# Modulation weight units of a two-layer diffusion backbone: in rows at four places, or one by one among gates, merge and up projection

## The chip, the core and the metric

The kernel runs on one core of a Trainium2 chip. The metric is the device time of one execution in microseconds (us). The engines are TensorE (PE in the rows; PEld is its weight load), VectorE (DVE), ScalarE (ACT), GpSimd (POOL) and SyncE (SP, which issues nearly all DMAs). All arithmetic is float32; a matmul product is made from high and low parts in three terms (high x high, low x high, high x low), so every weight block of 512 KB is split once into `wh` (ScalarE) and `wl` (VectorE).

## The reference, cut to what matters

Six vectors per layer (shift, scale and gate of each of the two sub-layers) are a product of SiLU of the condition with `w_mod`, for the latent and for the context tokens. They depend on nothing else, so they can be computed at any time before their first use.

```python
for l in range(DEPTH):                                   # DEPTH = 2, 512 latent and 256 context tokens
    mod_l = jnp.split((silu_c @ w_mod[l] + b_mod[l])[:, None, :], 6, axis=-1)
    mod_c = jnp.split(silu_cc @ w_mod[l] + b_mod[l], 6, axis=-1)
    pl = split_proj(modulate(x, mod_l[0], mod_l[1]) @ w_in[l] + b_in[l])
    ...
    mix_l = gated_merge(pl[-1], yr_l, ya_l, ym_l, w_br_ret[l], w_br_att[l], w_br_mlstm[l], w_out[l])
    x = layer_norm(alpha * x + mod_l[2] * mix_l, ln1_g[l], ln1_b[l])
    ffn_l = conv_ffn(modulate(x, mod_l[3], mod_l[4]), w_up[l], conv_w[l], conv_b[l], w_down[l])
    x = layer_norm(alpha * x + mod_l[5] * ffn_l, ln2_g[l], ln2_b[l])
```

The context tokens go the same way in layer 0; in layer 1 only the latent tokens go past the mixers.

## The kernel before

**The modulation units.** `w_mod` of both layers is cut into 48 units (layer, which of the six vectors, which quarter). One unit (`mod_unit`, L332) loads two raw blocks of 512 KB from `wmod` and makes eight matmuls of 256 columns into the tile `pp`, four in each block, with the raw weights as the moving side and 32 columns of the condition (`silc`) as the fixed side. The result is copied by ScalarE (first of four units) or added by VectorE (the other three) into `part`, 128 x 256, L345 and L348. When four units are in `part`, the next unit, or a demand for one of the four, calls `flush_mod` (L319): two small matmuls into `pm` turn `part` into columns, and four VectorE instructions (L328) write them to `modc`. The first eight units run at the very start and in the first projection. The other 40 wait in the list `modq`, in the order of layer, vector and quarter. `tmod(l, idx, n)` (L353) takes up to n of them off the list if they are not past (l, idx); `need_mod` (L358) takes all up to (l, idx) and flushes.

**The order of the work.** TensorE's order is the order in which the program is written; the `Mixer` lets background generators (the scans, attention, `finish`, `gate_rows`) step in between the matmul groups of the foreground by an estimated clock. The order on the other engines and on SyncE's queue is made by a scheduler that keeps dependencies. Raw blocks lie in a ring of five buffers, split blocks in two pairs, PSUM in three banks for the long products (`g`) and five for everything else; each DMA on SyncE's queue waits in its turn for its buffer.

**The stages of a layer.** After the input projections and the scans, 24 gate blocks are projected and stored to DRAM (`dr_g`), with attention in the background. `merge` then runs for three branches, each with four weight blocks (`wbr`); its input, the tile pair `yh`, `yl`, is converted by `yprep` (L1290) from `dr_y` and lies in the same buffer as the input of the gate blocks. The output projection (`wout`) follows, and `finish` (L1045) normalises tile by tile in the background: VectorE and ScalarE make `xn`, then `post` (L1049) transposes it on TensorE (`ptr`) and `to_xT` (L409) modulates it and splits it into `xh` and `xl`, the input of the next projection. The up projection (`wup`, 44 blocks in four groups; context tokens first in the first group) goes through the convolution to `ah`, `al`, and the down projection (`wdn`) of a group follows. A second `finish` makes the input of layer 1.

**Where the 40 units stand.** Eight one by one in the input stage (L1254, L1262, L1269); four at the start of the merge of layer 0 (L1371); in `post` of each of the six tiles two units ahead of the transposes, in the first `finish` of layer 0 (twelve units) and in the second (twelve); in `post` of each of the four tiles of layer 1's first `finish` one unit (four). The numbers stand in the last argument of `finish`: the first two name the vectors that must be there, the other three are the arguments of `tmod`. The `tmod` in the up projection (L1431) finds nothing left that it may take.

Of the kernel before, what the change touches and what calls it, by code (L numbers as in the profile page):

```python
# [149 lines left out]
class Mixer:  # L150
    """Emits the steps of a foreground and of queued background generators in one TensorE order."""

# [51 lines left out]
def _program(es, nc, tc, I, OUT):  # L204
    V, S, G, SP = nc.vector, nc.scalar, nc.gpsimd, nc.sync
    M = Mixer()
# [51 lines left out]
    modc = [ctile([128, 6, 8, 2], f"modc{l}") for l in range(DEPTH)]  # L258
# [786 lines left out]
    def finish(key, X, xslot, gname, bname, l, tiles, emit, xT=None, mc=None, sidx=0, mi=None):  # L1045
# [3 lines left out]
        def post(t, xn):  # L1049
            need_mod(*mi[:2])  # L1050
            tmod(*mi[2:])
            to_xT(xn, t, xT[0], xT[1], mc, sidx, int(t >= 4))
            M.done.add(f"{key}.{t}")
# [55 lines left out]
    def layer(l, xT, key):  # L1109
        last = l == DEPTH - 1  # L1110
# [170 lines left out]
        for f in range(24):  # L1281
            def ev(g, a, b):
                t = stg()
                S.activation(t[:, :b - a], g, AF.Tanh, scale=0.5, bias=bh[:, B_G + f:B_G + f + 1])
                SP.dma_start(out=dr_g[f][:, a:b], in_=t[:, :b - a])
            yield from fm(wblock(I["wfm"][l, B_G - 1 + f]), xh, xl, qseg, ev)

        yh, yl = new_xT()
# [34 lines left out]
        def merge(bi, segs):  # L1323
# [3 lines left out]
            for q in range(4):  # L1327
                blk = wblock(I["wbr"][l, bi, q])
                if bi == 0 and q == 1:
                    yprep(1)  # L1330
                if bi == 1 and yold:
                    yatt_load(yold.pop(0))
                    if yold:
                        yatt_load(yold.pop(0))
# [30 lines left out]
        hT = None  # L1365
# [4 lines left out]
        yprep(0)  # L1370
        tmod(0, 4, 4)  # L1371
        yield from merge(0, qseg)
# [5 lines left out]
        for pi, ats in enumerate(aparts):  # L1378
# [4 lines left out]
            if pi == 0:  # L1383
                X = (zt if last else Xt())[:, :6144].rearrange("p (t c) -> p t c", t=6)
                yield f"g2{l}"
                hT = (yh, yl) if last else new_xT()
                M.add(finish(key, X, xslot, "ln1_g", "ln1_b", l, lt, None, hT, modc[l], 3, (l, 4, 1, 5, 1) if last else (0, 4, 1, 1, 2)), [f"a{l}"])
            for ts in ((ats,) if last else trips):
# [22 lines left out]
        for gr, (go, gnum) in enumerate(zip(GOFF, GROUPS)):  # L1411
# [4 lines left out]
            for pi, segs in enumerate(passes):  # L1416
# [3 lines left out]
                for jn, j in enumerate(range(go, go + gnum)):  # L1420
# [3 lines left out]
                    for half, jj in enumerate((j, NF + j)):  # L1424
# [4 lines left out]
                        tt.append(t)  # L1429
                        if gr and not last:  # L1430
                            tmod(1, 1)  # L1431
                    if cut:
# [13 lines left out]
            if final:  # L1446
# [5 lines left out]
                else:  # L1452
# [3 lines left out]
                    nx = new_xT()  # L1456
                    M.add(finish(key2, X, xslot, "ln2_g", "ln2_b", l, lt, emit, nx, modc[l + 1], 0, (1, 1, 1, 4, 2)))
            if gr == 0:
# [59 lines left out]
```

## Time and profile before

| what | value |
|---|---|
| time, median of three runs | 2564.7 us (2563.7 to 2565.76) |
| span of the profiled execution | 2558.8 us |
| TensorE busy | 2467.1 us, 96% |
| VectorE busy | 1585.4 us, 62% |
| ScalarE busy | 1005.9 us, 39% |
| moved by DMA | 329.21 MB, mean 129 GB/s |

The span goes from the first to the last instruction of one profiled execution; what lies around it is in the time but not in the span. The busy shares are means over stages that differ, so they are read stage by stage: a stretch in which TensorE has no gap, and one in which it waits for another engine, say different things about the same instruction.

### The profile page before, as it was taken

To read this page: it belongs to the slowest core of one execution; us is meant where nothing else is said; L and a number is where in the kernel's file an instruction comes from. 1 tells how busy PE (TensorE), PEld (TensorE's weight loads), DVE (VectorE), ACT (ScalarE), POOL (GpSimd) and SP (SyncE) were. 2 spreads that over 40 slices of the span, in tenths; PEclk is the share of its full clock that TensorE was granted. 3 is DMA by queue.
4 is the path that set the end of the run, shared out by engine and by line. 5 is a ranking of instruction groups with operands and counts; after the bars stand their busy time and mean duration, and the time that the engine had idled before them with its cause. 6 is when DMAs were issued, how large, how long until landed. Compare 5 with 4: busy or idle time off the path is not lost.

```text
span 2558.8 us, 41711 instructions
## 1 busy us (share of the span) xinstructions
PE 2467.1 (96%) x16552; PEld 2163.6 (85%) x16552; DVE 1585.4 (62%) x3338; ACT 1005.9 (39%) x1802; POOL 92.3 (4%) x111
## 2 busy tenths in 40 slices
PE   6999999999899989999999989999999998999998
PEld 4877898888788978999898978778887888988887
DVE  5555465554476885455545684756665778855557
ACT  4422321454443464232313253433245455633332
POOL 1000001000000000000000010000110000000000
PEclk9999999999999999999999999999999999999999
DMA  7343434322454662212121375243443444533232
GB/s 254 102 164 120 144 102 138 113 81 81 150 185 132 227 239 83 83 46 79 54 74 59 95 276 170 91 153 126 158 140 123 139 158 162 182 107 99 83 104 70
DMA packets 147651, 329.21 MB, mean 129 GB/s; under 512 B 15872, under 2 KB 59136, under 8 KB 147456
## 3 DMA queue, kind: packets, MB, share of 16 engines
q1 hardware_dynamic: 147456, 326.54, 38.2%
q8 instruction: 131, 2.15, 0.3%
q14 instruction: 64, 0.52, 0.1%
HBM read 283.49 MB, written 42.99 MB: 128 GB/s over the span
## 4 chain that ended last, share of the span: by engine, by line
PE 86%; DVE 6%; DMA 3%; ACT 3%; issue 1%; POOL 0%; SPq 0%; DVEq 0%; ACTq 0%; POOLq 0%
PE g L214 72%; PE psc L214 2%; PE pAV L214 2%; PE pPT L218 2%; DVE wl L314 1%; PE pNb L214 1%; PE pNf L214 1%; PE pE L214 1%; ACT wh L313 1%; PE pp L214 1%; PE pU L214 1%; PE pO L214 1%; DMA raw<-in_wtm_dram 1%; DMA raw<-in_wmod_dram 1%; DMA stg<-dr_y 1%
## 5 line engine op out<-in xcount | busy, mean ns | idle before, releaser
L214 PE MATMUL g<-xh,wh 128*128 128x512 f32 (+1 forms) x2448 | 825.6, 352 | 11.3 <-ACT xh L1295 5.0
L214 PE MATMUL g<-xl,wh 128*128 128x512 f32 (+1 forms) x2448 | 812.0, 347 | 4.8 <-DVE xl L426 3.7
L314 DVE TENSOR_TENSOR wl<-raw,wh 128x1024 fp32r<-128x1024 f32 (+3 forms) x358 | 411.9, 1151 | 355.7 <-ACT wh L313 267.3
L313 ACT CAST wh<-raw 128x1024 fp32r<-128x1024 f32 (+3 forms) x358 | 355.5, 993 | 609.3 <-PE g L214 550.9
L214 PEld LDWEIGHTS g<-xh,wh 128*128 128x128 f32 x2448 | 465.0, 190 | 82.4 <-issue 12.9
L214 PEld LDWEIGHTS g<-xl,wh 128*128 128x128 f32 x2448 | 465.7, 190 | 61.1 <-DVE xl L426 4.2
L214 PE MATMUL g<-xh,wl 128*128 128x512 f32 (+1 forms) x2448 | 510.2, 347 | 3.0 <-DVE wl L314 3.0
L214 PEld LDWEIGHTS g<-xh,wl 128*128 128x128 f32 x2448 | 401.1, 190 | 61.4 <-DVE wl L314 3.6
L214 PE MATMUL g<-wh,ah 128*128 128x256 f32 x808 | 207.2, 284 | 3.6 <-ACT ah L1439 3.6
L214 PE MATMUL g<-wh,al 128*128 128x256 f32 x808 | 206.4, 283 | 2.7 <-DVE al L1440 2.7
L214 PE MATMUL g<-wh,xh 128*128 128x256 f32 (+1 forms) x768 | 201.1, 292 | 3.0 <-ACT wh L313 2.3
L214 PE MATMUL g<-wh,xl 128*128 128x256 f32 (+1 forms) x768 | 196.8, 287 | 1.6 <-DVE xl L426 1.5
L214 PEld LDWEIGHTS g<-wh,ah 128*128 128x128 f32 x808 | 153.1, 189 | 4.9 <-ACT ah L1439 4.2
L214 PEld LDWEIGHTS g<-wh,al 128*128 128x128 f32 x808 | 153.0, 189 | 4.1 <-DVE al L1440 3.5
L214 PEld LDWEIGHTS g<-wh,xh 128*128 128x128 f32 x768 | 149.0, 194 | 7.6 <-ACT wh L313 2.7
L214 PEld LDWEIGHTS g<-wh,xl 128*128 128x128 f32 x768 | 149.0, 194 | 2.4 <-DVE xl L426 1.9
L1400 ACT ACTIVATE tc<-g,conv 128x512 f32<-128x512 f32 (+1 forms) x142 | 97.0, 683 | 136.8 <-PE g L214 134.9
L927 ACT ACTIVATE Pe<-psc,mx 128x256 f32<-128x256 f32 (+1 forms) x144 | 80.9, 566 | 168.2 <-DVE mx L922 115.9
L214 PE MATMUL g<-wl,ah 128*128 128x256 f32 x808 | 144.0, 281 | 1.3 <-DVE wl L314 1.3
L1401 DVE SCALAR_TENSOR_TENSOR tc<-g,conv,tc 128x511 f32<-128x511 f32 (+1 forms) x142 | 88.7, 625 | 84.5 <-ACT tc L1400 83.9
L398 POOL TENSOR_TENSOR rstd<-veps,mhalf 128x1 f32<-128x1 f32 (+3 forms) x68 | 71.7, 1057 | 1823.4 <-DVE veps L396 1745.9
L214 PE MATMUL g<-wl,xh 128*128 128x256 f32 (+1 forms) x768 | 127.8, 287 | 0.9 <-DVE wl L314 0.8
(279 smaller groups left out, 3199.9 us busy)
## 6 DMA issues: line engine op xcount, KB each, us to landing
raw<-in_wup_dram SPq DMA_DIRECT2D x108, 512.0 KB, 3.5
raw<-in_wmod_dram SPq DMA_DIRECT2D x96, 512.0 KB, 5.4
raw<-in_wfm_dram SPq DMA_DIRECT2D x80, 512.0 KB, 3.4
raw<-in_wtm_dram SPq DMA_DIRECT2D x32, 512.0 KB, 5.1
raw<-in_wout_dram SPq DMA_DIRECT2D x32, 512.0 KB, 3.9
raw<-in_wbr_dram SPq DMA_DIRECT2D x28, 512.0 KB, 3.8
dr_g<-stg SPq DMA_DIRECT2D x48, 256.0 KB, 2.0
raw<-in_wdn_dram SPq DMA_DIRECT2D x20, 512.0 KB, 3.5
```

Source lines behind the costliest of these rows:

```text
L214: nc.tensor.matmul(out, lhsT, rhs, **kw)
L218: nc.tensor.transpose(out, in_, ident)
L313: S.copy(h[:, :n], raw[:, :n])
L314: V.tensor_tensor(l[:, :n], raw[:, :n], h[:, :n].bitcast(F32), op=OP.subtract)
L398: G.tensor_tensor(r, t, mhalf[:, :n], op=OP.pow)
L927: S.activation(pe[:, a:b], prs[si][:, :b - a], AF.Exp, bias=mx[:, 3:4], scale=0.125, accum_out=sm[:, si:si + 1])
L1400: S.activation(t[:, a:b], g, AF.Identity, bias=conv[:, jj, 3:4], scale=conv[:, jj, 1:2])
L1401: V.scalar_tensor_tensor(t[:, a + 1:b], g[:, :b - a - 1], conv[:, jj, 0:1], t[:, a + 1:b], op0=OP.mult, op1=OP.add)
```

## The change

The units behind the first eight that stood in rows are taken one at a time. One is taken after every third gate block of layer 0 (eight), one ahead of every second weight block of a merge of layer 0 (six), and one after each pair of up projection blocks in the groups 1 to 3 of layer 0 (seventeen); the last unit remains for `need_mod` in `gate_rows` of layer 1. The row at the start of the merge and those in `post` are gone. The eight units of the input stage stay.

```diff
@@ class Mixer
-    """Emits the steps of a foreground and of queued background generators in one TensorE order."""
+
@@ finish, post
-            need_mod(*mi[:2])
-            tmod(*mi[2:])
+            need_mod(*mi)
             to_xT(xn, t, xT[0], xT[1], mc, sidx, int(t >= 4))
@@ layer, gate blocks
             yield from fm(wblock(I["wfm"][l, B_G - 1 + f]), xh, xl, qseg, ev)
+            if f % 3 == 2:
+                tmod(0, 5)
@@ layer, merge
                     yprep(1)
+                if not last and q % 2 == 1:
+                    tmod(1, 5)
                 if bi == 1 and yold:
@@ layer, before the first merge
         yprep(0)
-        tmod(0, 4, 4)
         yield from merge(0, qseg)
@@ layer, first finish
-                M.add(finish(key, X, xslot, "ln1_g", "ln1_b", l, lt, None, hT, modc[l], 3, (l, 4, 1, 5, 1) if last else (0, 4, 1, 1, 2)), [f"a{l}"])
+                M.add(finish(key, X, xslot, "ln1_g", "ln1_b", l, lt, None, hT, modc[l], 3, (l, 4)), [f"a{l}"])
@@ layer, up projection
                         tt.append(t)
-                        if gr and not last:
-                            tmod(1, 1)
+                    if gr and not last:
+                        tmod(1, 5)
@@ layer, second finish
-                    M.add(finish(key2, X, xslot, "ln2_g", "ln2_b", l, lt, emit, nx, modc[l + 1], 0, (1, 1, 1, 4, 2)))
+                    M.add(finish(key2, X, xslot, "ln2_g", "ln2_b", l, lt, emit, nx, modc[l + 1], 0, (1, 1)))
```

Three places show how instructions move. TensorE, the start of layer 0's merge, before: `pAV` is the last piece of background attention after the gate blocks, `pp` and `pm` are units and a flush, and the first `g` belongs to the merge.

```order
L218 MATMUL pPT<-ident,Pe 128x128 x6
L214 MATMUL pAV<-PT,va 64x128 x12
L214 MATMUL pp<-raw,silc 32x256 x8
L214 MATMUL pm<-selm,part 128x8 x2
L214 MATMUL pp<-raw,silc 32x256 x24
L214 MATMUL g<-xh,wh 128x512
L214 MATMUL g<-xl,wh 128x512
```

The same place in the changed kernel (the first `g` rows are the end of the last gate block):

```order
L214 MATMUL pAV<-PT,va 64x128 x12
L214 MATMUL g<-xh,wh 128x256
L214 MATMUL g<-xl,wh 128x256
L214 MATMUL g<-xh,wh 128x256
L214 MATMUL g<-xl,wh 128x256
L214 MATMUL g<-xh,wl 128x256 x8
L214 MATMUL pp<-raw,silc 32x256 x8
L214 MATMUL g<-xh,wh 128x512
L214 MATMUL g<-xl,wh 128x512
```

One unit is left between the gates and the merge instead of four, and the flush is gone from there. TensorE, the first tile of layer 0's first `finish`, before: output projection, flush and two units, transposes, output projection.

```order
L214 MATMUL g<-wl,zh 128x256 x4
L214 MATMUL pm<-selm,part 128x8 x2
L214 MATMUL pp<-raw,silc 32x256 x16
L218 MATMUL ptr<-ident,xn 128x128 x8
L214 MATMUL g<-wh,zh 128x256
```

The same place in the changed kernel:

```order
L214 MATMUL g<-wh,zl 128x256
L214 MATMUL g<-wl,zh 128x256 x4
L218 MATMUL ptr<-ident,xn 128x128 x8
L214 MATMUL g<-wh,zh 128x256
L214 MATMUL g<-wh,zl 128x256
```

The transposes now follow the projection directly; so at all 16 tiles. VectorE, the last tile of layer 0's first `finish`, before: `mod` modulates the tile, the two `xl` finish it, `wl` and `tc` belong to the up projection, and `dg` are the diagonal products for the second gate.

```order
L421 TENSOR_SCALAR mod<-ptr,modc_83 128x128 x4
L314 TENSOR_TENSOR wl<-raw,wh 128x1024
L1435 TENSOR_TENSOR tc<-tc 128x256
L314 TENSOR_TENSOR wl<-raw,wh 128x1024
L426 TENSOR_TENSOR xl<-mod,xh 128x4x128
L373 TENSOR_TENSOR dg<-ident,modc_83 128x512 x4
L426 TENSOR_TENSOR xl<-mod,xh 128x4x128
```

The same place in the changed kernel:

```order
L421 TENSOR_SCALAR mod<-ptr,modc_83 128x128
L1404 SCALAR_TENSOR_TENSOR tc<-g,conv,tc 128x255
L314 TENSOR_TENSOR wl<-raw,wh 128x1024
L426 TENSOR_TENSOR xl<-mod,xh 128x4x128 x2
L373 TENSOR_TENSOR dg<-ident,modc_83 128x512 x4
L1403 SCALAR_TENSOR_TENSOR tc<-g,conv,tc 128x255
```

The four `dg` now stand behind both `xl`, and one `wl` fewer ahead of them.

## Rows read from the trace of the kernel before

**Rows 1.** Page, head and part 1: span; engine, busy us (share of span), instructions.

```profile
span 2558.8 us, 41711 instructions
...
PE 2467.1 (96%) x16552; PEld 2163.6 (85%) x16552; DVE 1585.4 (62%) x3338; ACT 1005.9 (39%) x1802; POOL 92.3 (4%) x111
```

**Rows 2.** Windows: stretch, us, busy us per engine (instructions), granted clock, DMA share, GB/s.

```profile
871.06:905.40 34.34, 33.95 (x335) 30.30 (x333) 30.14 (x78) 19.77 (x35) 4.12 (x5) 1.00 0.61 221
905.40:953.47 48.07, 41.61 (x367) 37.29 (x365) 44.49 (x103) 38.31 (x73) 4.62 (x6) 0.93 0.78 280
1011.00:1430.00 419.00, 419.00 (x2773) 386.18 (x2772) 220.11 (x299) 125.31 (x160) 0.74 (x1) 1.00 0.21 67
1470.60:1547.40 76.80, 63.53 (x584) 54.11 (x582) 60.91 (x156) 44.71 (x88) 12.16 (x20) 0.96 0.83 287
2134.60:2190.00 55.40, 50.36 (x427) 46.29 (x425) 48.75 (x112) 36.50 (x64) 3.76 (x5) 0.97 0.59 204
```

**Rows 3.** Windows of the tile `pp` alone: PE, PEld, DVE and ACT as above.

```profile
871.06:905.40 34.34, 6.01 (x96) 2.70 (x96) 1.60 (x4) 0.74 (x2) 1.00 0.61 221
905.40:953.47 48.07, 6.01 (x96) 2.70 (x96) 2.12 (x5) 0.37 (x1) 0.93 0.78 280
1470.60:1547.40 76.80, 12.32 (x192) 5.24 (x192) 3.66 (x9) 1.11 (x3) 0.96 0.83 287
2134.60:2190.00 55.40, 4.28 (x64) 1.67 (x64) 1.26 (x3) 0.37 (x1) 0.97 0.59 204
```

**Rows 4.** Timeline of TensorE, input stage: start, length, instruction, idle time before it.

```profile
176.29 1.07 PE L214 MATMUL pp<-raw,silc 128*32 128x256 f32 x16
...
177.76 0.48 PE L214 MATMUL g<-xh,wh 128*128 128x512 f32 x1
```

**Rows 5.** Line 348, who waited for the sum (us, times).

```profile
  PE pm L214: 1.8, 2
```

**Rows 6.** Waits of TensorE, 1430 to 1560 us: total, times, longest us.

```profile
PE ptr L218 <- ACT xn L1082: 8.2, 4, 4.7
PE g L214 <- ACT wh L313: 2.3, 2, 2.1
...
PE g L214 <- ACT ah L1439: 1.2, 1, 1.2
PE g L214 <- DVE al L1440: 1.0, 1, 1.0
PE pp L214 <- DMA raw<-in_wmod_dram: 0.6, 1, 0.6
```

**Rows 7.** Timeline of TensorE, start of layer 0's merge.

```profile
685.70 1.07 PE L214 MATMUL pp<-raw,silc 128*32 128x256 f32 x16
...
693.61 1.08 PE L214 MATMUL pp<-raw,silc 128*32 128x256 f32 x8 [4.87 <-DMA raw<-in_wmod_dram]
695.05 2.25 PE L214 MATMUL pp<-raw,silc 128*32 128x256 f32 x16 [0.36 <-DMA raw<-in_wmod_dram]
698.74 0.80 PE L214 MATMUL g<-xh,wh 128*128 128x512 f32 x1 [1.43 <-ACT wh L313]
...
703.28 0.48 PE L214 MATMUL g<-xh,wh 128*128 128x512 f32 x1
```

**Rows 8.** Timeline of TensorE, start of layer 1's merge.

```profile
1976.45 0.50 PE L214 MATMUL g<-xh,wh 128*128 128x512 f32 x1 [1.28 <-ACT xh L1295]
...
1981.96 0.79 PE L214 MATMUL g<-xh,wh 128*128 128x512 f32 x1 [3.68 <-ACT xh L1295]
```

**Rows 9.** Timeline of VectorE, one flush.

```profile
871.60 0.37 DVE L328 SCALAR_TENSOR_TENSOR modc<-pm,bmod 128x4 f32<-128x4 f32 x4 [0.29 <-PE pm L214]
```

**Rows 10.** Timeline of TensorE, first matmul on the last tile, layer 0.

```profile
953.47 0.50 PE L214 MATMUL g<-xl,wh 128*128 128x512 f32 x1 [2.53 <-DVE xl L426]
```

**Rows 11.** Timeline of VectorE, ahead of that matmul.

```profile
950.32 2.49 DVE L373 TENSOR_TENSOR dg<-ident,modc 128x512 f32<-128x512 f32 x4
952.73 0.69 DVE L426 TENSOR_TENSOR xl<-mod,xh 128x512 fp32r<-128x512 f32 x1
```

**Rows 12.** Timeline of ScalarE, second LayerNorm of layer 0.

```profile
1513.31 1.04 ACT L313 CAST wh<-raw 128x1024 fp32r<-128x1024 f32 x1 [6.97 <-DMA raw<-in_wtm_dram]
1514.26 0.72 ACT L1076 ACTIVATE xn<-xres,nm 128x512 f32<-128x512 f32 x1
```

**Rows 13.** Timeline of VectorE, same place.

```profile
1514.39 1.23 DVE L314 TENSOR_TENSOR wl<-raw,wh 128x1024 fp32r<-128x1024 f32 x1 [3.81 <-ACT wh L313]
```

## The prediction, made before the changed kernel was run

> **What bounds the kernel now.** I read the page's busy times first, then the execution cut into stretches, then the wait lists and the engines' order of time inside the stretches that the change touches. TensorE is busy 2467.1 of the 2558.8 us span [rows 1], so all its gaps together are 91.7 us, and a change that moves TensorE work about without removing any can only make these gaps smaller or larger. The stretches differ: in the up and down projections of layer 0, from 1011 to 1430 us, TensorE is busy 419.00 of 419.00 us and VectorE 220.11; in the four stretches where a LayerNorm finishes, VectorE is busy 30.14 of 34.34, 44.49 of 48.07, 60.91 of 76.80 and 48.75 of 55.40 us [rows 2]. So the normalising stretches are paced mostly by VectorE (88, 93, 79 and 88%), and the projections by TensorE alone. The reader is to see in these rows that a TensorE instruction costs its full length in the second kind of stretch and may cost nothing in the first, where TensorE waits for VectorE's results anyway.
>
> **The change, part by part.** No work is removed: the same 40 modulation units run after the first eight. 32 of them change place. Now four stand at the start of layer 0's merge, six and six in the two stretches of layer 0's first LayerNorm, twelve in its second, four in layer 1's first (16 matmul records are one unit, so 96, 96, 192 and 64 records [rows 3]). Afterwards eight stand between gate blocks, six in the merges, seventeen in the up projections of layer 0, and one is left over and runs when layer 1 asks for the last gate.
>
> *What the new places cost.* A lone unit takes 1.07 us, and a unit with the flush behind it 1.47 us from its start to the next matmul, so the flush is 0.4 [rows 4]. Gates, merges and projections leave TensorE no gap to put it in, so 31 units and 8 flushes cost 31 x 1.07 + 8 x 0.4 = 36.4 us. Their DMA is hidden there: two loads of 512 KB come per two or three weight blocks, and the DMA share of the projections is 0.21 [rows 2]; if that cover were gone, the price is one wait as at the merge start now, 4.87 us, at each place. On VectorE each unit adds at most one sum of about 0.41 us (3.66 us for nine [rows 3]) where VectorE is half idle: nothing. The SyncE queue gets the loads between those of the weight blocks; a load that waits for one of the five raw buffers holds the gate rows queued behind it, but that buffer was read two or three weight blocks earlier: nothing. The unit left over costs 1.07 + 0.4, and its flush stands directly behind it, so TensorE waits for the sum; the two cases of that wait took 1.8 us together [rows 5], so 0.9 more: 2.4 us (between 1.5, where other matmuls get between, and 3.3). Against this, one unit now falls into the gap between the up and the down projection of the last group of layer 0, where TensorE waited 1.2 and 1.0 us for the two halves of the activation [rows 6]: minus 1.0 (between 0 and 2.2). Cost: 36.4 + 2.4 - 1.0 = 37.8 us.
>
> *Merge start.* From 685.70 to 698.74 us TensorE does four units and otherwise waits, 4.87, 0.36 and 1.43 us, for the units' loads and for the merge weights queued behind them; eight records then take 1.08 us where sixteen took 1.07, the lower of the two clock levels (1.2 instead of 2.4 GHz), which lasts to 703.28 [rows 7]. 13.0 us, and half of the 4.5 us at the low clock, 2.3, leave: 15.3. But these units also cover the conversion of the branch outputs, which cannot start before the last gate matmul, since both use the same buffer. Layer 1 has no units at that place and shows what is then late: TensorE waits 1.28 and 3.68 us for ScalarE's conversion [rows 8]. With the low clock that follows such a wait (2.3 as above), rounded down because one unit still stands ahead of it, I put 7 back. Recovered: 8.3 us (between 5, where the wait is as long as the present waits and their low clock, 10, and 13, where the one unit left ahead of it covers nearly all).
>
> *First LayerNorm of layer 0* (871 to 953 us). If VectorE paces it, only VectorE's own work counts: the sums, 1.60 + 2.12 us [rows 3], and three flushes at 0.37 [rows 9], 4.8 us. The last wait, 2.53 us [rows 10], goes too: four diagonal products, 2.49 us [rows 11], stand ahead of the last half of the last tile and in the new order behind it. 4.8 + 2.5 = 7.3. Bounds: 4.8, and the 12 units' whole TensorE time with that wait, 12 x 1.07 + 3 x 0.4 + 2.5 = 16.5.
>
> *Second LayerNorm of layer 0* (1471 to 1547 us). Here VectorE is busy only 79%, and the DMA share is 0.83 [rows 2]. VectorE's work falls by 3.66 [rows 3] + 1.1 = 4.8. Loads explain more: ScalarE stood 6.97 us before a weight block of layer 1, queued behind modulation loads, and the tile's statistics waited behind it [rows 12]; VectorE lost 3.81 us by it [rows 13]. TensorE's own waits for such blocks and for a unit's load are 2.1 and 0.6 [rows 6]. Without 24 loads of 512 KB I count all three gone: 4.8 + 3.8 + 2.7 = 11.3. Bounds: 4.8, and 12 x 1.07 + 3 x 0.4 + 3.8 + 2.7 = 20.5. The 8.2 us that TensorE waits for normalised tiles [rows 6] do not go; they grow, since units now stand in front of some of these waits.
>
> *First LayerNorm of layer 1* (2135 to 2190 us). Four units, 4.28 us [rows 3], two flushes. VectorE loses 1.26 + 0.37 = 1.6 us of work, TensorE 5.1; half the units follow long runs of matmuls and come back whole, the others fall into waits: 3.4 with the second flush (between 1.6 and 5.1).
>
> *Sum.* Cost 37.8, recovered 8.3 + 7.3 + 11.3 + 3.4 = 30.3, so 7.5 us longer. The profiled execution spans 2558.8 us, and the median of the three timed runs is 2564.7, 5.9 more for what lies outside the span, which the change doesn't touch: 2558.8 + 7.5 + 5.9 = 2572.2 us.
>
> **The rivals.** *Faster, 2552.1 us.* The normalising stretches are paced by TensorE and by loads, and VectorE just follows. Then every unit's time comes back there: 8.3 + 16.5 + 20.5 + 5.1 = 50.4 against 37.8, minus 12.6. For it: the DMA shares of 0.61 to 0.83 there against 0.21 in the projections [rows 2]. Against it: TensorE already waits for normalised tiles behind a pair of units (8.2 us in the second LayerNorm [rows 6]), and a pair taken away ahead of such a wait only lengthens it. It decides if the three LayerNorms give back over 29.5 instead of 22 us. The Trainium skill (Perfetto Trace Analysis, section Optimization Strategy) says that where the most contended engine changes over time, interleaving those regimes may improve performance; by that rule the load-heavy units belong among the long projections, and the time would be this rival's. The trace agrees that the regimes differ, but shows the contended engine of the normalising stretches to be VectorE, from which the units take little.
>
> *No difference, about 2565.* Half of the above: the loads hold up more of the chain of tiles than the two waits that I counted, and the LayerNorms and the merge start give back between 32.7 and 42.9 us.
>
> *Much slower, about 2586 us.* The chain of tiles doesn't move except for VectorE's removed work, and the merge start waits as long as it does now: recovered 5 + 4.8 + 4.8 + 1.6 = 16.2, against 37.8: 21.6 more. For it: VectorE at 93% between 905 and 953 us [rows 2]; against it: the 3.81 us idle behind one late block [rows 13].
>
> That the units are not spread at all is no case of weight: in the new order each stands alone between matmuls.
>
> **How the numbers follow.** A measurement of this kernel tells about 0.2%, 5.1 us, from no change. Chances: forecast 0.43 (its own range 2569 to 2578), no difference 0.30, faster rival 0.16, much slower 0.11. Slower by over 0.2% is 0.43 + 0.11 = 0.54. The range goes from 2558, which leaves most of the faster rival's gain outside, to 2582, which leaves out the far half of the much slower one; together less than 2 in 10. It holds the bounds of the second LayerNorm, the widest ones: with 20.5 there instead of 11.3 the time is 2563, with 4.8 it is 2578.7.
>
> **What would show it.** In the new profile the projections of layer 0 should be longer by some 17 units, about 20 us, with TensorE still without gaps; the waits for normalised tiles should be longer than now, in the second LayerNorm well over 8.2 us; the merge start should show a wait for the conversion of branch outputs like layer 1's, and the second LayerNorm no 7 us wait of ScalarE for a block. Wrong would be: LayerNorm stretches shorter by the whole time of their units (then TensorE paced them), or TensorE waits for modulation loads in the projections.

## The result and the profile after

The changed kernel takes 2583.4 us (median; 2578.9 to 2584.0), the kernel before 2564.2 us in the same comparison: a ratio of 1.0072, with a 95% interval of 1.0058 to 1.0086. It is slower, by about 18.5 us by the ratio, where 7.5 were forecast; the time lies 1.4 us above the range. The profiled execution of the changed kernel spans 2577.1 us, 18.3 more than before.

The page of the changed kernel, head and busy times (engine, busy us, share of the span, instructions), against [rows 1]:

```profile
span 2577.1 us, 41702 instructions
...
PE 2474.3 (96%) x16552; PEld 2166.3 (84%) x16552; DVE 1585.7 (62%) x3338; ACT 1008.1 (39%) x1802; POOL 93.5 (4%) x111
```

TensorE's gaps grew from 91.7 to 102.8 us, 11.1 more, and its busy time by 7.2, from 2467.1 to 2474.3 us; both together are the 18.3 us. TensorE's instructions are the same in number. The mean granted clock fell from 0.989 to 0.987 of full speed, which is about 5 us more lost to the low clock, a part of them in waits, where they cost nothing. The rest of the busy time fits units that stand alone and take somewhat longer than the 1.07 us they were priced at: in the projections, which have neither gaps nor low clock, sixteen of them cost 1.7 us more than forecast (table below).

The five stretches of [rows 2] in the changed kernel (stretch, us, busy us of PE, PEld, DVE, ACT and POOL with instructions, granted clock, DMA share, GB/s), from about the same matmul to about the same matmul (the edges are off by up to 3 us, and the third stretch ends 10 us early):

```profile
885.00:919.70 34.70, 32.10 (x261) 31.90 (x260) 30.55 (x72) 22.09 (x39) 3.69 (x5) 0.95 0.30 100
919.70:965.80 46.10, 35.32 (x256) 33.92 (x255) 41.41 (x93) 34.10 (x64) 4.83 (x6) 0.89 0.36 115
1021.00:1450.00 429.00, 429.00 (x2983) 385.93 (x2982) 219.43 (x320) 123.00 (x159) 0.74 (x1) 1.00 0.31 105
1497.40:1564.00 66.60, 52.18 (x389) 50.63 (x388) 58.46 (x139) 46.31 (x85) 11.89 (x19) 0.90 0.54 179
2150.20:2207.60 57.40, 47.31 (x359) 45.54 (x357) 47.27 (x105) 36.30 (x63) 4.48 (x5) 0.94 0.42 139
```

The projections stay without a gap and their DMA share rises from 0.21 to 0.31. In the four LayerNorm stretches TensorE's work falls and VectorE stays busy nearly as long as before: 41.41 of 46.10 us (90%) and 58.46 of 66.60 us (88%, where it was 79%). Their clock is lower than before (0.95 for 1.00, 0.89 for 0.93, 0.90 for 0.96, 0.94 for 0.97), and TensorE waits more there. What the forecast named as signs came: the projections grew by about 20 us without a gap, ScalarE no longer waits for the load of a weight block in the second LayerNorm, and TensorE waits 13.9 us for normalised tiles there, where it waited 8.2 [rows 6] (what it waited for, total, times, longest):

```profile
PE ptr L218 <- ACT xn L1081: 13.9, 4, 5.7
```

To set forecast against measurement, the next table goes from a foreground matmul to the same one in both traces, at the times of the kernel before. Stretches in which a kernel has no edit differ by up to 3 us between the traces (one, early in layer 1, by up to 7; it has its own place in the last section), so nothing under 3 us is read from one row alone.

| stretch (us, before) | what it holds | forecast | measured |
|---|---|---|---|
| 410 to 874 | gates and merges of layer 0: 14 units and 4 flushes in, row out | +8.3 | +15.1 |
| 874 to 1012 | first LayerNorm of layer 0 | -7.3 | -5.4 |
| 1012 to 1430 | up projections: 16 units, 4 flushes | +18.7 | +20.4 |
| 1430 to 1470 | gap to the down projection, one unit | +0.1 | -2.8 |
| 1470 to 1585 | second LayerNorm of layer 0 | -11.3 | -13.0 |
| 1585 to 2134 | layer 1, no edit | 0 | +1.7 |
| 2134 to 2300 | first LayerNorm of layer 1, late unit | -1.0 | +3.1 |
| the rest | | 0 | -0.7 |
| sum (rounded) | | +7.5 | +18.3 |

Two rows are off to the bad side by more than the traces differ: gates and merges by 6.8 us, layer 1's LayerNorm by 4.1. Here is TensorE at the start of layer 0's merge in the changed kernel, with one late ScalarE instruction and SyncE's queue around it (start, length, engine, instruction; in brackets the idle time before it and what ended it), against [rows 7]:

```profile
700.58 1.07 PE L214 MATMUL pp<-raw,silc 128*32 128x256 f32 x16
703.20 0.49 PE L214 MATMUL g<-xh,wh 128*128 128x512 f32 x1 [1.55 <-ACT xh L1296]
704.19 0.79 PE L214 MATMUL g<-xl,wh 128*128 128x512 f32 x1 [0.50 <-DVE xl L1297]
...
710.44 0.80 PE L214 MATMUL g<-xh,wh 128*128 128x512 f32 x1 [4.58 <-ACT xh L1296]
...
709.56 0.83 ACT L1296 CAST xh<-stg 128x768 fp32r<-128x768 f32 x1 [5.68 <-DMA stg<-dr_y]
...
702.65 0.38 SPq L1284 DMA_DIRECT2D dr_g<-stg  x1
704.17 1.39 SPq L1295 DMA_DIRECT2D stg<-dr_y  x2
```

The row is gone, and with a last wait of 0.20 TensorE waits 6.8 us there, where it waited 6.7 before. The waits for the units' loads became waits for the branch outputs: two of the four loads are issued only at 704.17, behind the store of the last gate from a staging buffer (702.65), and the first of them is there for ScalarE at 709.56.

And layer 1's first LayerNorm in the changed kernel, TensorE behind the first transposed tile:

```profile
2156.54 0.39 PE L214 MATMUL g<-wh,xh 128*128 128x256 f32 x1 [1.73 <-ACT xh L1359]
...
2158.48 0.58 PE L214 MATMUL g<-wh,xl 128*128 128x256 f32 x1 [1.56 <-DVE xl L1360]
```

These two waits, for the high and low halves of the merge output, are not among the waits of the kernel before.

### The profile page after: what moved, and what is told of

It reads as the page before. It is cut to its first block, busy times and chain, and to the rows that moved or that the text cites. A ratio compares the mean times of both kernels' runs of the same rounds, so it can differ in the third digit from the quotient of the medians.

```text
span 2577.1 us, 41702 instructions
## 1 busy us (share of the span) xinstructions
PE 2474.3 (96%) x16552; PEld 2166.3 (84%) x16552; DVE 1585.7 (62%) x3338; ACT 1008.1 (39%) x1802; POOL 93.5 (4%) x111
## 4 chain that ended last, share of the span: by engine, by line
PE 85%; DVE 7%; DMA 3%; ACT 3%; issue 1%; POOL 0%; SPq 0%; DVEq 0%; ACTq 0%; POOLq 0%
PE g L214 71%; PE pAV L214 2%; PE psc L214 2%; DVE wl L314 2%; PE pPT L218 2%; PE pp L214 1%; PE pNb L214 1%; PE pNf L214 1%; DMA stg<-dr_y 1%; PE pE L214 1%; PE pU L214 1%; ACT wh L313 1%; PE pO L214 1%; PE ptr L218 1%; PE pyt L218 0%
```

## The experiments

The theory that I went in with (called A at first): the rows stood in time in which TensorE waits anyway, at the borders of stages, for conversions by ScalarE and VectorE; taken away they free little and cost their full length elsewhere. The rival: the forecast's own prices, with an error somewhere else. Each run is compared with the kernel before in its own session. The changed kernel has the four executions of the first comparison alone, so between it and another kernel a difference under some 0.2%, 5 us, is not clear of noise; what is said of single stretches comes from one trace of each kernel.

### Each row put back into the changed kernel

Four runs undo one place each. Units are handed out in a fixed order, so what a place takes back the projections lose.

```
merge_row_back:    if f % 6 == 2: tmod(0, 5)       # gates: 4 units, not 8
                   yprep(0); tmod(0, 5, 4)          # row of 4
ln1_rows_back:     no units in the merges; LN1 of layer 0 takes 2 at each tile
ln2_rows_back:     projections only up to (1, 2); LN2 takes 2 at each tile
layer1_posts_back: projections up to (1, 4); layer 1's LN1 takes 1 at each tile
```

> The changed kernel with one part undone: four of the eight units between the gate blocks of layer 0 stand in a row at the merge start again, the rest stays spread. Theory A (the row stood in time in which TensorE waits anyway: in the changed kernel the merge start still waits 1.55, 0.50, 4.58 and 0.20 us without it): four units and a flush, 4.7 us, leave the gates, and the merge start grows by 1 to 3 us for them; so 2 to 4 us faster than the changed kernel, ratio to the kernel before 1.0056 to 1.0064. Theory B (the forecast's own term, the row costs 8.3 us at the merge start): 3.6 us slower than the changed kernel, ratio about 1.0086.

Measured: 2587.5 us, ratio 1.0090 (1.0076 to 1.0104), 4.6 us slower than the changed kernel by the ratios, whose intervals overlap. That is theory B's number, and theory A's lies outside the interval, but the trace does not show theory B's reason. Its TensorE, at the merge start and behind it:

```profile
702.83 0.64 PE L214 MATMUL pp<-raw,silc 128*32 128x256 f32 x8 [3.04 <-DMA raw<-in_wmod_dram]
...
708.14 0.80 PE L214 MATMUL g<-xh,wh 128*128 128x512 f32 x1 [1.29 <-ACT wh L313]
...
727.37 0.61 PE L214 MATMUL pm<-selm,part 128*128 128x8 f32 x4 [1.48 <-ACT Pe L927]
```

The row's waits are back (3.04, 0.69, 0.98 and 1.29 us), and of the branch outputs' waits two small ones are left (0.41 and 0.20). So the merge start waits 6.6 to 6.8 us with the row and without it. What the trace has more are waits for the attention outside that place, 5.1 us in all for 2.9, the longest two for the softmax (`Pe`), 2.07 and 1.48 us, each with low clock behind it; the changed kernel has 1.07, 0.63, 0.60 and two small ones. Another 3 us lie between 1585 and 1976 us, without an edit there.

> The changed kernel with one part undone: no units in the merges, the twelve units in the two stretches of the first LayerNorm of layer 0 are back, two at each tile; the up projections of layer 0 take twelve instead of seventeen, none is left for layer 1. Theory A (most of the units there stand beside waits for normalised tiles; the changed kernel's trace shows the stretch giving back only 5.6 us): 11 units and 3 flushes leave TensorE-bound places (13.0), the late unit goes (2.4), 5.6 come back: about 9.8 us faster than the changed kernel, ratio 1.0034, with the waits for the normalised tiles short again (3.6, 0.3 and 2.5 us instead of 8.8, 2.6 and 1.1). Theory B (TensorE and loads pace the stretch, so the units cost their whole 16.5 there): 1 us slower, ratio 1.0076.

Measured: 2582.0 us, ratio 1.0068 (1.0056 to 1.0081), no difference to the changed kernel that can be told. By stretch: the LayerNorm takes 7.5 us more with its twelve units than the changed kernel has without (forecast 7.3), so that term was right and theory A wrong. The merges give back 3.5 us for six units, since a wait of 2.43 us for the attention appears; and layer 1 from 1585 to 1976 us, which has no edit, is 7.2 us longer (more on that in the last section).

> The changed kernel with one part undone: the twelve units in the second LayerNorm of layer 0 are back, two at each tile; the up projections of layer 0 take six instead of seventeen, none is left for layer 1. Theory A (loads hold up this stretch, so it costs 13.6 us as read from the changed kernel's trace): 11 units and 3 flushes less in the projections (13.0), late unit gone (2.4), 13.6 back: 1.8 us faster than the changed kernel, ratio 1.0065, and ScalarE again waits some 7 us for a weight block of layer 1. Theory B (the units stood in waits there too, and only VectorE's 4.8 us count): 10.6 us faster, ratio 1.0031.

Measured: 2581.2 us, ratio 1.0062 (1.0048 to 1.0075), as theory A said (here it is that the loads hold up the stretch). The twelve units cost 11.8 us in this LayerNorm (1.2 less than before with them, 13.0 less without; the forecast had 11.3), and ScalarE's wait for a weight block of layer 1 is back, 9.9 us in three, the longest 6.2.

> The changed kernel with one part undone: four units stand in the first LayerNorm of layer 1 again, one at each tile; the up projections of layer 0 take fourteen instead of seventeen and none is left over. Theory A (the units there covered the conversion of the merge output, which now shows as waits of 1.73 and 1.56 us): three units and a flush less in the projections (3.6), the late unit gone (2.4), and the LayerNorm stretch 2 us shorter than without them: 8 us faster than the changed kernel, ratio 1.0041. Theory B (the forecast's term: they cost 3.4 us there): 2.6 us faster, ratio 1.0062.

Measured: 2585.5 us, ratio 1.0079 (1.0066 to 1.0091). Both theories fall: the units stand at each tile as in the kernel before, and still the stretch from 2134 to 2300 us is 4.9 us longer than there.

### Gates, and the planner's price

```
gates_free:        no tmod between the gates;
                   projections: tmod(1, 5, 2 if jn % 2 == 0 else 1)
after_unit_price:  M.cost(-2.4)  ->  M.cost(-5.9)
```

> The changed kernel with the eight units between the gate blocks of layer 0 moved on to the up projections of layer 0 (every other place there takes two); merges as in the changed kernel, no row at the merge start. Theory A (the forecast's price: a unit between gate blocks costs its own 1.07 us and a share of a flush): the stretch from the gates to the first LayerNorm is 8 x 1.07 + 2 x 0.4 = 9.4 us shorter than in the changed kernel, the projections 9.4 to 10.3 longer, the whole within 1 us of the changed kernel (ratio to before 1.0072). Theory B (units there cost more, since they push the attention's and retention's steps into each other): that stretch at least 13 us shorter, the whole 3 us or more faster, ratio 1.0060 or less.

Measured: 2594.9 us, ratio 1.0110 (1.0093 to 1.0127). The stretch from the gates to the LayerNorm is 6.3 us shorter than in the changed kernel and the projections 8.7 longer: nearer to theory A, the forecast's price of 9.4, than to theory B, and less than either. The whole is slower than either theory had it, because no unit is left for the gap to the down projection (2.8 us) and two units fall back into the first LayerNorm (4.2). From the gates to the end of the merges TensorE now waits 7.2 us for attention steps, where the changed kernel waits 2.9, at one place 3.65 us:

```profile
720.16 0.44 PE L218 MATMUL pPT<-ident,Pe 128*128 128x128 f32 x2 [3.65 <-ACT PT L944]
```

> The changed kernel with one number changed: the planner that mixes attention and retention steps into the foreground counts 1.06 us for a modulation unit instead of 4.56 (its matmuls' 6.96 minus a refund of 2.4, now 5.9). Theory B (the counted price made the background run ahead: 44 more background matmuls stand before the same foreground matmul at 600 us than in the kernel before): the new waits in the gates (1.07, 0.63, 0.21 us) go and the stretch from gates to first LayerNorm is 2 to 6 us shorter than in the changed kernel, ratio 1.0050 to 1.0064. Theory A: no difference there, ratio 1.0072.

Measured: 2599.9 us, ratio 1.0131 (1.0113 to 1.0148); theory B falls, with the sign reversed, and theory A's "no difference" with it. The background now runs more than 100 matmuls behind that of the kernel before, and what is left of it stands close together in the merges, where TensorE waits for its steps (2.63 and 2.38 us, and shorter ones). The high price was no mistake that costs time. But the run shows how much hangs on this mixing: 11 us between 410 and 874 us, with no unit moved.

### The buffers at the merge start

```
after_yprep_ring, before_yprep_ring:  t = St("yp") if k > 1 and bi == 0 else stg()
after_yprep_all:                      t = St("yp") if bi == 0 else stg()
before_last_output:                   t = St("yp") if bi == 0 and last and k == 3 else stg()
```

> The changed kernel; at the start of each layer's merge the third and fourth of the four branch outputs are loaded into buffers of another ring than the three staging buffers. Theory A (what took the place of the row at the merge start is the ring of three: the third load could only be issued when a conversion or the last gate's store had freed a buffer, and TensorE waited 4.58 us): the wait shrinks to under 1 us in layer 0 and the wait of 3.68 us in layer 1 as well, 4.6 + 3.7 and 2 to 5 us of low clock, so 8 to 12 us faster than the changed kernel, ratio 1.0025 to 1.0040. Rival (the loads wait for the branch outputs themselves, or for the queue): within 2 us of the changed kernel, ratio 1.0065 or more.

> The changed kernel with all four branch outputs of each merge start loaded into the other ring (the run with two of them only moved the wait to the one load that still had to wait for a staging buffer). Theory A (one late load made the 4.58 us wait): in layer 0 the waits at the merge start fall from 6.8 to 3 to 5 us, for conversions alone, and the low clock there shortens by 2 us or more; in layer 1 the waits of 1.28 and 3.68 us fall by 2 us or more; 4 to 8 us faster than the changed kernel, ratio 1.0040 to 1.0056. Rival (conversions alone make the wait, in whichever buffer): within 2 us, 1.0065 or more.

Measured: 2580.5 us, ratio 1.0054 (1.0041 to 1.0068), and 2574.7 us, ratio 1.0045 (1.0031 to 1.0059). The first lies between theory A and the rival: with two outputs in the other ring the long wait in layer 0 stays (4.44) and the one ahead of it grows from 1.55 to 3.31, since one load is still issued behind the store of the last gate, at 703.58; with all four the waits fall from 6.8 to 5.3 us, and in layer 1 the 3.68 us wait goes (the stretch is 5 us shorter). The kernel is 7 to 9 us faster than the changed one. So the ring of three was the cause of the long wait in layer 1 and of a part of that in layer 0.

> The kernel before, in which only layer 1's last branch output of the merge start is loaded into the other ring; all orders elsewhere are those of before. If the wait of 3.68 us there came from the ring of three staging buffers, it shrinks to under 1 us and the low clock behind it shortens: 3 to 5 us faster, ratio 0.9980 to 0.9988. If not: ratio 1.0000.

Measured: 2565.9 us, ratio 1.0004 (0.9995 to 1.0014); the wait is 3.13 us. One buffer is not enough: of the other three loads the last is still issued behind the store of the last gate.

> The kernel before with the same edit: third and fourth branch output of each merge start into another ring. Its modulation units stay where they were. Layer 1's wait of 3.68 us at the merge start should go (3.7 us and some 2 us of low clock), in layer 0 the row of units waits for its own loads, so 0 to 2 us there. Against it: the program that orders VectorE's and SyncE's instructions gives another order in the first LayerNorm of layer 1 here, as it does in all kernels with moved units, and there all these kernels lose 3 to 5 us. If that loss has to do with the order and not with the units, it shows here too, though no unit is moved: ratio 0.9985 to 1.0005 in all, and 3 to 5 us more between 2134 and 2240 us. If it has to do with the units: no loss there, ratio 0.9965 to 0.9985.

Measured: 2570.6 us, ratio 1.0018 (1.0005 to 1.0032), slower than either case had it. The merge start of layer 1 is some 3 us shorter, as expected. Here no unit is moved, TensorE's order in layer 1 is that of before, and the stretch from 2134 to 2300 us is 6.7 us longer. TensorE in it:

```profile
2141.12 0.39 PE L214 MATMUL g<-wh,xh 128*128 128x256 f32 x1 [0.41 <-ACT xh L1356]
2142.03 0.38 PE L214 MATMUL g<-wh,xl 128*128 128x256 f32 x1 [0.53 <-DVE xl L1357]
2143.41 0.58 PE L214 MATMUL g<-wh,xh 128*128 128x256 f32 x1 [1.00 <-ACT xh L1356]
2145.31 0.58 PE L214 MATMUL g<-wh,xl 128*128 128x256 f32 x1 [1.32 <-DVE xl L1357]
```

layer1_posts_back has the same four waits: 0.77, 0.53, 0.99 and 1.31 us. What differs is the order of VectorE and SyncE, which the kernel doesn't fix by hand as it does TensorE's. VectorE first in the kernel before, then in this one, some 19 us ahead of these waits:

```profile
2122.37 0.69 DVE L1302 TENSOR_TENSOR xl<-pAV,xh 128x512 fp32r<-128x512 f32 x1
2122.97 0.20 DVE L1073 TENSOR_SCALAR nm<-lnsum 128x1 f32<-128x1 f32 x1
...
2122.41 0.21 DVE L1073 TENSOR_SCALAR nm<-lnsum 128x1 f32<-128x1 f32 x1
2122.58 0.69 DVE L1302 TENSOR_TENSOR xl<-pAV,xh 128x512 fp32r<-128x512 f32 x1
```

From there the two kernels do the merge's sums, the splits of weight blocks and the splits of the merge output in different orders, and VectorE waits 2.12 us for gate rows at 2134.32. That TensorE comes there 3 us earlier is not the reason by itself: in before_gap_outputs below it comes 6 us earlier and the LayerNorm is no longer than before.

### Single parts of the change in the kernel before

```
before_row_early:   first four gate projections: tmod(0, 4, 2); no row
before_merge_units: merges take 6 units; LN1 of layer 0 takes 1 at each tile
before_posts_moved: four units in the up projections; none in layer 1's LN1
```

> The kernel before with one part of the change alone: the four units at layer 0's merge start run earlier, two instead of one at the four first places after the gate projections of layer 0; the order in layer 1 stays that of before. The early places cost 4 x 1.07 + 0.4 = 4.7 us, up to 5.1. Forecast's term (the row costs 8.3 us more than what takes its place): 3.2 to 3.6 us faster than before, ratio 0.9986. Theory A (the waits for the branch outputs take the place of the row's waits and low clock in full, only the units' own 4.7 us come back): within 1 us of before, ratio 1.0000. Theory C (the units in the row stood in time that is waited anyway, nothing comes back): 4 to 5 us slower, ratio 1.0018.

Measured: 2568.6 us, ratio 1.0014 (1.0003 to 1.0026): slower by 3.6 us, for an early cost of 4.7 to 5.1. So the row's removal gave back 1.1 to 1.5 us (1.3 by the stretch from 410 to 874 us; by the interval of the ratio, anything from -2 to 4), between theories A and C and nearer to C, and 8.3 is out. TensorE in place of [rows 7]:

```profile
692.06 0.49 PE L214 MATMUL g<-xh,wh 128*128 128x512 f32 x1 [1.04 <-ACT xh L1295]
693.05 0.49 PE L214 MATMUL g<-xl,wh 128*128 128x512 f32 x1 [0.50 <-DVE xl L1296]
695.56 0.80 PE L214 MATMUL g<-xh,wh 128*128 128x512 f32 x1 [2.01 <-ACT xh L1295]
696.55 0.80 PE L214 MATMUL g<-xl,wh 128*128 128x512 f32 x1 [0.20 <-DVE xl L1296]
698.01 0.80 PE L214 MATMUL g<-xh,wh 128*128 128x512 f32 x1 [0.66 <-ACT xh L1295]
699.00 0.80 PE L214 MATMUL g<-xl,wh 128*128 128x512 f32 x1 [0.20 <-DVE xl L1296]
...
714.20 0.58 PE L214 MATMUL psc<-KH,Qe 128*128 128x256 f32 x1 [2.18 <-DVE Qe L904]
```

Six waits for conversions, 4.6 us, then 2.18 us for an attention step whose operands the shorter merge start no longer covers (and 0.47 for a later one): 7.3 us for 6.7, and a second stretch at the low clock: 6.8 us are lost to it in the gates and merges, where it was 5.1. Only the units' own 4.7 us leave, and the rest eats most of them.

> The kernel before with one part of the change alone: six of the twelve units of layer 0's first LayerNorm stand in the merges of layer 0 as in the changed kernel, the LayerNorm keeps one at each tile; the row at the merge start and layer 1's order stay. Theory A (forecast's prices: 6 x 1.07 and a flush in the merges, half of 7.3 back in the LayerNorm): merges 6.8 to 7.6 us longer, LayerNorm 3 to 4 shorter, ratio 1.0012 to 1.0018. Theory B (units between the merge blocks also shift the attention's steps, which TensorE then waits for, 1.5 to 4 us with the low clock behind it): merges 9 us longer or more, ratio 1.0020 or more.

Measured: 2569.2 us, ratio 1.0021 (1.0012 to 1.0030), theory B at its lower end. The stretch from 410 to 874 us is 10.4 us longer for six units and two flushes (7.2 by the forecast's prices). In it TensorE waits 4.2 us for attention steps, where the kernel before waits 2.1: the two longest grow from 0.90 and 0.82 to 1.32 and 2.20. The LayerNorm gives 2.8 back. The two waits in the kernel before, and the first of them here:

```profile
764.07 0.41 PE L218 MATMUL pPT<-ident,Pe 128*128 128x128 f32 x2 [0.90 <-DVE Pe L935]
789.53 0.65 PE L214 MATMUL pAV<-PT,va 128*64 128x128 f32 x6 [0.82 <-ACT PT L944]
...
762.21 0.44 PE L218 MATMUL pPT<-ident,Pe 128*128 128x128 f32 x2 [1.32 <-DVE mx L924]
```

> The kernel before with one part of the change alone: the four units in layer 1's first LayerNorm run in the up projections of layer 0 instead, one in each of four places; the order of VectorE's merge work in layer 1 is that of before up to the first normalised tile. Projections: 4 x 1.07 + 0.4 = 4.7 to 5.2 us longer. Theory A (these units cost 3.4 us in the LayerNorm, as the forecast said, and the loss there in the other kernels comes from another order of VectorE and SyncE alone): 3 to 4 us come back between 2134 and 2240 us, ratio 1.0004 to 1.0008. Theory B (they covered the conversion of the merge output): nothing comes back or the stretch gets up to 2 us longer, ratio 1.0018 to 1.0028.

Measured: 2575.2 us, ratio 1.0040 (1.0025 to 1.0055): theory B and more. VectorE's order is that of before up to the first normalised tile, no unit stands in the LayerNorm, and the stretch from 2134 to 2300 us is 2.1 us longer, where the forecast's term would have it 3.4 shorter. TensorE's waits there are those of the changed kernel:

```profile
2151.87 0.39 PE L214 MATMUL g<-wh,xh 128*128 128x256 f32 x1 [1.94 <-ACT xh L1356]
2153.14 0.39 PE L214 MATMUL g<-wh,xl 128*128 128x256 f32 x1 [0.89 <-DVE xl L1357]
```

So the first unit and its flush did cover the conversion of the merge output. The projections take 5.2 us more, as expected; another 5.2 us lie between 1585 and 1976 us, without an edit there.

### The one place that came out better

```
before_gap_unit:    after the last up projection of layer 0: tmod(1, 4)
before_gap_outputs: the same, and t = St("yp") if bi == 0 else stg()
```

> The kernel before with one unit of layer 0's second LayerNorm moved into the gap between the last up projection and the down projection of layer 0. By the changed kernel's trace that stretch gets 2.8 us shorter with one unit more in it (gaps of 2.2 us filled, low clock of 1.7 gone), where the forecast counted 1.0 against a unit's 1.07; the LayerNorm gives back 0.5 to 1.3 for one unit less. Against it: VectorE's order in layer 1 is another one here, worth 3 to 6 us in the other kernels. So 2.8 us less between 1430 and 1470 us, 3 to 6 more between 2134 and 2240, ratio 0.9995 to 1.0010. If the forecast's size is right, nothing changes between 1430 and 1470 us, ratio 1.0005 to 1.0020.

Measured: 2552.8 us, ratio 0.9963 (0.9949 to 0.9977), faster than either case had it. The gap's stretch is 2.6 us shorter, as expected; the second LayerNorm gives back 6.8 us for one unit, not 1; and layer 1 loses nothing, though VectorE's order there is yet another one. TensorE's waits from the gap to the end of the second LayerNorm (what it waited for, total, times, longest), against [rows 6]:

```profile
PE ptr L218 <- ACT xn L1082: 5.0, 3, 1.9
PE pm L214 <- DVE veps L396: 2.1, 1, 2.1
PE g L214 <- DVE wl L314: 1.7, 3, 0.8
```

The waits for `ah` and `al` are gone, and the 4.7 us wait for a normalised tile is down to 1.9: ScalarE, which computes the tile, waited 9.5 us in all for weight blocks of layer 1 in the kernel before, and waits 5.6 here. One unit's loads less stand among those blocks; that this is the reason, and not the shifted order, no run shows by itself.

> The kernel before with the gap unit and all branch outputs of the merge starts in the other ring. From the parts: 2.8 to 3.8 us less at the gap and the second LayerNorm, 5 us less at layer 1's merge start (as in the changed kernel with the same edit), 0 to 2 less in layer 0, and 0 to 6 more in layer 1's first LayerNorm, depending on the order there, which is another one again. Ratio 0.9960 to 0.9990 if the parts add up; 1.0000 or more if the LayerNorm takes it all back.

Measured: 2549.7 us, ratio 0.9949 (0.9936 to 0.9961), some 13 us faster than the kernel before and about 32 faster than the changed one. That is more than its range allowed, since the gap's share was put at 2.8 to 3.8 us there. The measured parts, 9 us from the unit and 6.1 from layer 1's shorter merge start, add up to within 2 us.

## Why the prediction was off

**The direction and the theory of prices were right; three terms of the sum were not.** The late unit, the projections, and the first and second LayerNorm of layer 0 came out within 2 us of the forecast, and the runs with the rows put back confirm both LayerNorms (7.5 for 7.3, 11.8 for 11.3). The faster rival, which let every unit come back whole there, is out. The much slower rival comes nearest in number (2586 us) and is half right: its merge start, which waits as long as before, is what was measured, but its LayerNorms, which give back only VectorE's removed work, are not. The Trainium skill's rule that stood behind it (Perfetto Trace Analysis, section Optimization Strategy, on interleaving regimes with different contended engines) brought a gain at one place only, the gap to the down projection, where TensorE itself was idle; spread through the projections, where TensorE has no idle time, the units added their whole length (20.4 us for sixteen and four flushes).

**The step that failed first: "Recovered: 8.3 us" at the merge start.** The forecast let 15.3 us leave and put back 7, taken from layer 1's two waits [rows 8]. The run without the row (before_row_early) shows 7.3 us of waits in layer 0 and more low clock, not less: all of the row's waits come back under other names, the units' own 4.7 us are what leaves, and 1.1 to 1.5 remain. In the changed kernel 6.8 us of waits replace 6.7. I had the right mechanism and counted it at half its size: layer 0 has attention steps in that place that layer 1's rows could not show. The lower bound of 5 was a slip too: the row's waits and their low clock are 4.87 + 0.36 + 1.43 + 2.3 = 9.0 us and not 10, which makes it 6.3; what was measured lies below either.

**The price of the places between gates and merges** was put at a unit's own length, "no gap to put it in", and nothing was said of the background. Taking the eight units out of the gates gave back 6.3 us of 9.4, since longer waits for the attention take their place; the merges were dearer (10.4 for 7.2 in the single-part run). Outside the merge start the kernel before waits 2.1 us in all for attention steps from 430 to 866 us; the changed one 2.9, ln1_rows_back 4.1, before_merge_units 4.2, merge_row_back 5.1, gates_free 7.2. Of the 6.8 us by which this stretch was missed in the changed kernel, 3.6 are the row (4.7 leave instead of 8.3), 0.6 are more waits in all, and 2.6 are TensorE busy for longer than the units' prices, with the low clock alike in both (5.1 us lost). Of the 2.6, 14 x 0.1 would be the longer lone unit, by the 1.7 us that sixteen of them were dearer in the projections; the rest stays open.

**First LayerNorm of layer 1: "3.4" came out as a loss.** The forecast counted which units follow long runs of matmuls, and not what the first unit and flush covered: the conversion of the merge output, 3.3 us of waits once they are gone (1.73 and 1.56; 1.94 and 0.89 in before_posts_moved). Beside it the forecast took the other engines' order for unchanged where the diff changes nothing. It isn't: with no unit moved, another order of VectorE and SyncE cost 6.7 us here in before_yprep_ring and nothing in before_gap_unit. How much of the changed kernel's loss is cover and how much order stays open: in before_posts_moved the cover goes while VectorE's order still is that of before, but behind the first tile the order differs there too.

**The gap to the down projection was worth more than forecast**: 2.2 us of waits and the low clock behind them go, for a unit of 1.07 us, where I took 1.0 off. Alone, in the kernel before, the move gave 9 us, more than the gap holds: the rest came in the LayerNorm behind it, 6.8 us, probably by one unit's loads less in its queue.

**The low clock behind a wait was counted at the merge start only.** In all the changed kernel lost about 5 us more to it than the kernel before, most of it in the three LayerNorms.

## What to carry to other kernels

Work that stands where an engine waits may be free there; before moving it, ask what will be late next at that very place, and look for the answer in that place's own chain, not in a similar one. Moving a filler into an engine's real gap can be worth more than its length, and one such move can beat a scheme that moves them all. And where a program orders the other engines' queues, a move in one layer reorders them in another: allow some microseconds to either side for that.

## What the runs showed of the hardware

The same wait can cost very different amounts. Early in layer 1 TensorE waits 2.93 to 2.99 us for one weight block, at the same matmul in all seventeen traces. Windows of 20 us around it, in the kernel before and then in before_posts_moved (columns as above; the clock is the third number from the end):

```profile
1620.00:1640.00 20.00, 17.04 (x92) 14.09 (x91) 14.89 (x31) 11.74 (x21) 0.00 (x0) 1.00 0.40 124
1640.00:1660.00 20.00, 20.00 (x120) 17.57 (x119) 13.82 (x40) 8.39 (x17) 0.00 (x0) 1.00 0.33 108
...
1620.00:1640.00 20.00, 17.03 (x68) 13.61 (x67) 14.23 (x31) 7.21 (x11) 0.00 (x0) 0.79 0.43 131
1640.00:1660.00 20.00, 20.00 (x103) 17.09 (x103) 12.94 (x36) 7.88 (x16) 0.00 (x0) 0.95 0.27 80
```

Before, the granted clock is 1.00, the 2.4 GHz level, through and behind the wait; in the other kernel it is 0.79 and 0.95 in the two windows, that is, TensorE stands at 1.2 GHz for 10.2 us from about the end of the wait on, and 5 us are lost. ln1_rows_back and after_yprep_ring lost 7 us there, the changed kernel 1.7. In after_yprep_ring the clock stayed at 1.2 GHz through 13 us in which TensorE was busy for 12.94. What decides it the runs don't show; it is the 5 to 7 us that stayed unexplained between 1585 and 1976 us in several of the experiments. A part of the clock changes from one execution of the same kernel to the next: over the 66 executions of the kernel before that go with the experiments, the mean granted clock runs from 0.984 to 0.991 and the time from 2557.3 to 2571.9 us.
